# A two-layer decoder trunk on one core: both tiles' rotated transposes ahead of both splits, a longer softmax step, the residual loaded in eight pieces, and the first weights issued from ScalarE's queue

## The chip, the cores and the metric

The kernel runs on one core of a Trainium2 chip. The metric is the time of one execution in microseconds (us) on the device. The kernel before took 2349.48 us, the median of three runs (2347.7 to 2350.47).

## The reference

The program is a decoder trunk of two layers over a residual stream `x` of 256 rows by 2048 columns, in float32. The first layer uses differential attention with a partial rotary embedding, the second multi-head latent attention (MLA) with a separate rotated key. After each attention stands a cross-attention into 256 memory rows and an MLP with a squared ReLU. Each part starts with an RMS norm and ends with a residual addition.

```python
def partial_rope(x, cos, sin, rot):
    return jnp.concatenate([apply_rope(x[..., :rot], cos, sin), x[..., rot:]], axis=-1)

def diff_attention(h, wqkv, lam_vecs, subln, wo, cos, sin, lambda_init):
    q, k, v = jnp.split(h @ wqkv, 3, axis=-1)
    ...                                   # q, k: partial_rope, 16 half heads of 128
        s = jnp.where(causal_mask(q0, S), s, -jnp.inf)
        p = jax.nn.softmax(s, axis=-1)
        a = (p[:, :, 0] - lam * p[:, :, 1]).astype(v.dtype)
        return jnp.einsum('bhqk,bkhd->bqhd', a, v)

def mla_attention(h, wdown, q_norm, kv_norm, wuq, wukv, wo, cos, sin):
    d = h @ wdown
    c_q = rms_norm(d[..., :MLA_Q_LORA], q_norm)
    c_kv = rms_norm(d[..., MLA_Q_LORA:MLA_Q_LORA + MLA_KV_LORA], kv_norm)
    k_rope = apply_rope(d[..., MLA_Q_LORA + MLA_KV_LORA:][:, :, None, :], cos, sin)
    q = (c_q @ wuq).reshape(B, S, MLA_HEADS, MLA_NOPE + MLA_ROPE)
    q = jnp.concatenate([q[..., :MLA_NOPE], apply_rope(q[..., MLA_NOPE:], cos, sin)], axis=-1)
    ...                                   # k, v from c_kv, then softmax attention
```

## The kernel before

**Precision.** Each float32 operand is split into a rounded high part and a low part that is the rest. A product is three matmuls: high by high, high by low, low by high. For activations that come out of TensorE's transposes `split` makes the two parts: ScalarE casts the high part out of the result bank (L272), VectorE subtracts it from the bank to get the low part (L273).

**Weights.** They stream from HBM in tiles of 1 MB (`raw`), always loaded from SyncE's queue and in the order of the program. `split_weights` (L173) makes two halves of each: a cast on ScalarE gives `whi` (L187), a subtraction on VectorE `wlo` (L188). There are four `raw` buffers, which the tiles of the transposed input `xT` share at the start, and buffers of `whi` and `wlo` for two weight tiles. A half's cast therefore waits for the last matmul that reads the half two tiles earlier. `take` hands out the next weight tile, starts the load of a further one, and calls a hook if one is entered for the count of tiles taken so far.

**Matmuls.** `matmul_chunk` multiplies a chunk of four activation units by four weight tiles, into one result bank for each of the two row tiles of 128 rows (t = 0, 1). A weight tile is 24 matmuls of 128 x 512 (L155): two halves, two row tiles, six each. `w0`, `w1` and so on below are the weight tiles in the order of the stream; w0 to w3 give the first q chunk, w4 to w7 its k chunk, w8 to w11 its v chunk.

**Order.** TensorE runs its instructions in the order of the program. All else that it has to do (transposes L159, attention scores, products with the probabilities) is written as generators that `matmul_chunk` advances between its matmuls (`pump`), according to a planner's clock. A `yield` with a number of microseconds says when the next piece is due: `T_SM` (6.5) after a softmax, `T_ROT` (9.0) after a rotation, `T_TURN` (2.6) after a copy of transposed data. These figures are plans: they decide how many matmuls are put ahead of the next piece in TensorE's order, and how instructions are ordered on ScalarE, VectorE and GpSimd, each of which also works through its queue in order.

**The places that the change touches.**

- *Start.* SyncE loads `g`, then `xT` and w0 (in four pieces of 256 KB), w1, w2 between each other. `hooks[2] = first_norm` (L842) loads after the second tile the constants, both row tiles of `x` (1 MB each), positions and lambda vectors; ScalarE forms eight sums of squares (`sum_squares`, L301). From them come the scale of the norm (`rq`, `r1`) and, in `tables` (L677 to 707), the sine and cosine tables, of which sine needs another function table on ScalarE (L689).
- *Query heads of the first layer.* `project_diff` calls `heads_T` for each row tile: ScalarE evacuates and scales the bank (L354), GpSimd rotates a quarter of each head in six operations (`rope`, L365 to L370), TensorE transposes (L159), `split` makes the unit. In the code before, the scales and the tables are formed at the first of these calls.
- *Softmax step.* In `attend_diff` the difference of the two weighted probabilities `a` is formed on VectorE (L540, L541); after `yield T_SM + 1` TensorE transposes it (`prob_T`).
- *Rotated parts of MLA.* `shared_key` (one call) and `rotated` (in `project_latent`, one call for each of four head groups) rotate both row tiles, yield `T_ROT`, take a result bank `b`, and then do for each row tile in turn two transposes into its half of `b` and a `split` of that half.

Of the kernel before, what the change touches and what calls it, by code (L numbers as in the profile page):

```python
# [17 lines left out]
P = 128  # L18
D = 2048
S = 256  # L20
NT = 2
CH = 512
# [8 lines left out]
SC_DA = 1.0 / math.sqrt(128)  # L31
# [12 lines left out]
def trunk(ctx, tc, x, xT, mem, memT, positions, gcols, gfinal, lam_vecs, consts, W, out):  # L44
    nc = tc.nc
# [115 lines left out]
    def f32(ap):  # L161
        return ap.bitcast(F32)

    def load(dst, src):
        tc.keep_in_program_order(nc.sync.dma_start(dst, src))


    stream = []
# [1 line left out]
    def raw_tile():  # L170
        return wraw.tile([P, 4 * CH], F32, tag="raw", name=nm("raw"))

    def split_weights(src, width, pieces=2, loads=1):  # L173
        raw = raw_tile()
        n = 4 * width
        m = n // loads
        for i in range(loads):
            load(raw[:, i * m : (i + 1) * m], src[:, i * m : (i + 1) * m])
        m = n // pieces
        halves = []  # L180
        for i in range(pieces):
            at = i * m % (n // 2)
            if at == 0:
                halves.append([whalf.tile([P, 2 * CH], F32R, tag=tag, name=nm(tag)) for tag in ("whi", "wlo")])
            hi, lo = (w[:, at : at + m] for w in halves[-1])
            r = raw[:, i * m : (i + 1) * m]
            nc.scalar.copy(hi, r)  # L187
            nc.vector.tensor_tensor(lo, r, f32(hi), ALU.subtract)  # L188
        return halves

    plan = []
# [160 lines left out]
    def evacuate(ps, scale):  # L352
        e = work.tile([P, CH], F32, tag="ev", name=nm("ev"), bufs=6)
        nc.scalar.activation(e[:, : ps.shape[1]], ps, AF.Copy, scale=scale)  # L354
        return e
# [13 lines left out]
        e.tensor_tensor(a, m[0], m[1], ALU.subtract)  # L369
        e.tensor_tensor(b, n[0], n[1], ALU.add)  # L370

    def heads_T(ps, t, scale, dst, rot=None, spare=False):


        def task():
            e = evacuate(ps, scale)
            if rot:
                cos, sin, heads, half = rot
                rope(e.rearrange("p (h d) -> p h d", h=heads), cos, sin, heads, half)
            yield T_ROT if rot else T_EV  # L380
            b = ps
            if spare:
                b = yield from side_bank()
            split(dst, t, transpose4(e, b))
            if spare:
                give_back()
            yield T_TURN

        dst.run(task())
# [134 lines left out]
    def attend_diff(q, k, v, dst, coef, subcols):  # L524


        def block(t, heads, out):
            nk = (t + 1) * P
            sb = yield from side_bank()
            comps = [s for h in heads for s in (2 * h, 2 * h + 1)]  # L530
            scores(sb, [[(q, s, k[:, 0, s, :nk], k[:, 1, s, :nk])] for s in comps], nk, t, True)
            n = 2 * len(heads)
            pr, rs = softmax(sb, n)
            nc.vector.tensor_tensor(rs[:, :n], rs[:, :n], coef[:, :n], ALU.mult)
            a = work.tile([P, S], F32, tag="a", name=nm("a"))
            for i in range(len(heads)):
                p0 = pr[:, 2 * i * nk : (2 * i + 1) * nk]
                p1 = pr[:, (2 * i + 1) * nk : (2 * i + 2) * nk]
                ai = a[:, i * nk : (i + 1) * nk]
                nc.vector.tensor_scalar(ai, p1, rs[:, 2 * i + 1 : 2 * i + 2], None, ALU.mult)  # L540
                nc.vector.scalar_tensor_tensor(ai, p0, rs[:, 2 * i : 2 * i + 1], ai, ALU.mult, ALU.add)  # L541
            yield T_SM + 1
            pT = prob_T(a, 2, sb)
            give_back()
            yield T_TURN
            if not out:
                out.append((yield from side_bank()))
            po = out[0]
            nb = nk // P
            for i, h in enumerate(heads):  # L550
                for kb in range(nb):
                    blk = slice((i * nb + kb) * P, (i * nb + kb + 1) * P)
                    mm3(
                        po[:, h * S : (h + 1) * S], pT[:, 0, blk], pT[:, 1, blk],
                        val(v, 0, kb, h * S, S), val(v, 1, kb, h * S, S), kb == 0, kb == nb - 1,
                    )

        def normed(t, blocks, out):
            for b in blocks:
                yield b  # L560
            po = out[0]
            ss = small.tile([P, 2], F32, tag="ss2", name=nm("ss2"))
            for h in range(2):
                sum_squares(ss[:, h : h + 1], po[:, h * S : (h + 1) * S])
            r = rsqrt_mean(ss, 2, S)
            os = work.tile([P, CH], F32, tag="p", name=nm("os"), bufs=3)
            nc.vector.tensor_tensor(
                os.rearrange("p (h d) -> p h d", h=2), po.rearrange("p (h d) -> p h d", h=2),
                r[:, 0:2].unsqueeze(2).broadcast_to([P, 2, S]), ALU.mult,
            )  # L570
            yield T_NORM
            split(dst, t, scaled(transpose4(os, po), subcols))
            give_back()
            yield T_TURN

        def task():
            for i in q.tasks + k.tasks:
                yield i
            out = [[], []]
            b0 = Task(block(0, (0, 1), out[0]))  # L580
            yield 4.0
            b1 = Task(block(1, (0,), out[1]))
            n0 = Task(normed(0, [b0], out[0]))
            yield 4.0
            b2 = Task(block(1, (1,), out[1]))
            yield Task(normed(1, [b1, b2], out[1]))
            yield n0

        dst.run(task())
# [47 lines left out]


    load(g, gcols)
    warm = keep.tile([P, 1], F32, name="warm")  # L640
    nc.scalar.activation(warm, mhalf, AF.Exp)
    blank = work.tile([P, CH], mybir.dt.bfloat16, tag="junk", name="blank", bufs=1)
# [5 lines left out]
    norm = Stream(G_ATTN)  # L648
    for u in range(4):
        acts.append(given_unit(xT, u, G_ATTN))  # L650
        if u < 3:
            ready.append(split_weights(W["da_wqkv"][u], CH, 4 if u == 0 else 2, 4 if u == 0 else 1))
            plan.pop(0)
    posf = keep.tile([P, NT], F32, name="posf")
    cos = keep.tile([P, NT, NF], F32, name="cos")
# [8 lines left out]
    coef = keep.tile([P, 4], F32, name="coef")  # L664
    gsub = keep.tile([P, 4], F32, name="gsub")

    def first_norm():
        load(const, consts)
        for t in range(NT):
            load(xs[t], x[t * P : (t + 1) * P, :])  # L670
            for c in range(4):
                sum_squares(norm.ss[t][:, c : c + 1], xs[t][:, c * CH : (c + 1) * CH])
        load(pos, positions)
        load(lamv, lam_vecs)
        norm.rstd = [row_norm(norm.ss[t], D)[:, 0:1] for t in range(NT)]

    def tables():  # L677

# [160 lines left out]


    da_scales = []
    hooks[2] = first_norm  # L842

    hd = DA_ROT // 2

    def project_diff(gi):
        q, k, v = Held(unit()), Held(unit()), unit()
        for i, dst in enumerate((q, k)):
            ps = matmul_chunk(acts)
            if not da_scales:  # L850
                da_scales.append(keep2(norm.rstd, SC_DA, "rq"))
                da_scales.append(keep2(norm.rstd, 1.0, "r1"))
                tables()
            r = da_scales[i]
            for t in range(NT):
                heads_T(ps[t], t, r[t], dst, (cos[:, t, :hd], sin[:, t, :hd], 4, hd))
        ps = matmul_chunk(acts)
        for t in range(NT):
            values(ps[t], t, da_scales[1][t], v)
        return q, k, v  # L860
# [61 lines left out]
    def shared_key():  # L922
        for t in range(NT):
            e = ropes[t]
            rope(e[:, 0:1, 0:64], cos[:, t, hd:], sin[:, t, hd:], 1, hm)
            nc.vector.tensor_copy(e[:, 1, 64:128], e[:, 0, 0:64])
        yield T_ROT
        b = yield from side_bank()
        for t in range(NT):
            pt = b[:, 2 * t * P : 2 * (t + 1) * P]  # L930
            for i in range(2):
                flip(pt[:, i * P : (i + 1) * P], ropes[t][:, i, :])
            split(krope, t, pt.rearrange("p (k t) -> p k t", k=2))
        give_back()
        yield T_TURN

    def project_latent(gi):
# [3 lines left out]
        def rotated(ps):  # L941
            es = []
            for t in range(NT):
                e = evacuate(ps[t][:, :256], rq[t])
                rope(e[:, :256].rearrange("p (h d) -> p h d", h=4), cos[:, t, hd:], sin[:, t, hd:], 4, hm)
                es.append(e)
            yield T_ROT
            b = yield from side_bank()
            for t in range(NT):
                pt = b[:, 2 * t * P : 2 * (t + 1) * P]  # L950
                for i in range(2):
                    flip(pt[:, i * P : (i + 1) * P], es[t][:, i * P : (i + 1) * P])
                split(qr, t, pt.rearrange("p (k t) -> p k t", k=2))
            give_back()
            yield T_TURN

# [139 lines left out]
```

## Time and profile before

| | |
|---|---|
| median of the runs | 2349.48 us |
| the profiled execution | 2349.74 us |
| its span in the profile | 2348.0 us |
| mean granted TensorE clock | 0.992 |
| moved by DMA | 425.36 MB, mean 181 GB/s |

The profile is of one execution. Engines are PE (TensorE; PEld its weight loads), DVE (VectorE), ACT (ScalarE), POOL (GpSimd) and SP (SyncE). A row of the timeline gives the start in us from the start of the span, the duration, engine, line, operation, the tile written and the tile read with their sizes, and in brackets how long the engine was idle before and who released it. Several equal instructions in a row are put together (x4); their duration is then that of all. The chain of waits is followed back from the last instruction: its rows are start, duration, engine and line. The releaser is inferred, and where several semaphores were waited for, it is the one that came last in the records. PEclk is the share of TensorE's full clock that was granted.

### The profile page before, as it was taken

What the parts mean: (1) busy time and instruction counts of PE and PEld (TensorE: products, weight loads), DVE (VectorE), ACT (ScalarE), POOL (GpSimd) and SP (SyncE); (2) the same over time, 40 slices, a digit from 0 to 9 for tenths busy, and PEclk for the clock granted to TensorE, in tenths of its full rate; (3) what the DMA queues carried; (4) which work ended last, traced back from release to release, by engine and by line L of the source; (5) the groups of instructions that cost most, each with busy time, mean ns of one, the idle gap of its engine ahead of it and who ended that gap; (6) DMA issues with size and microseconds to landing.
All of it is one profiled execution on the core that took longest, in us unless ns stands there. A gap on an engine that the chain in (4) does not pass through costs nothing.

```text
span 2348.0 us, 27366 instructions
## 1 busy us (share of the span) xinstructions
PE 2306.8 (98%) x10860; PEld 1928.4 (82%) x10860; DVE 1302.3 (55%) x1502; ACT 1130.8 (48%) x1539; POOL 191.5 (8%) x258
## 2 busy tenths in 40 slices
PE   8999999999999999999999899999999999999998
PEld 6888787888888888888889688888888888888886
DVE  5665647774454454454556466777445445445454
ACT  6544545664434434434445455565443443443443
POOL 1111010001001000000001211000100100100111
PEclk9999999999999999999999899999999999999999
DMA  7455555545555555555545233554555555555553
GB/s 295 164 177 179 182 191 189 175 155 185 188 191 195 181 196 186 190 196 181 185 164 197 100 132 134 195 177 147 195 181 196 188 189 197 181 193 189 191 200 123
DMA packets 64353, 425.36 MB, mean 181 GB/s; under 512 B 7392, under 2 KB 7520, under 8 KB 15328
## 3 DMA queue, kind: packets, MB, share of 16 engines
q1 hardware_dynamic: 64224, 423.61, 53.0%
q8 instruction: 85, 1.39, 0.2%
q14 instruction: 44, 0.36, 0.0%
HBM read 421.48 MB, written 2.10 MB: 180 GB/s over the span
## 4 chain that ended last, share of the span: by engine, by line
PE 93%; DMA 2%; DVE 2%; ACT 1%; issue 1%; POOL 1%; SPq 0%; ACTq 0%; POOLq 0%; DVEq 0%
PE mm L155 88%; PE ax L155 2%; PE mm L159 2%; PE ax L159 1%; DVE wlo L188 1%; DMA memrow<-in_mem_dram 1%; ACT whi L187 1%; DMA x<-in_x_dram 0%; DMA raw<-in_da_wqkv_dram 0%; ACT junk L301 0%; DVE unit L295 0%; DVE unit L273 0%; DMA raw<-in_xT_dram 0%; POOL rope L367 0%; DMA raw<-in_memT_dram 0%
## 5 line engine op out<-in xcount | busy, mean ns | idle before, releaser
L155 PE MATMUL mm<-whi,unit 128*128 128x512 f32 (+2 forms) x6336 | 1978.2, 390 | 4.3 <-ACT whi L187 3.5
L188 DVE TENSOR_TENSOR wlo<-raw,whi 128x1024 fp32r<-128x1024 f32 (+2 forms) x794 | 962.6, 1213 | 943.9 <-ACT whi L187 943.0
L155 PEld LDWEIGHTS mm<-whi,unit 128*128 128x128 f32 x6336 | 1191.3, 189 | 242.6 <-ACT whi L187 4.8
L187 ACT CAST whi<-raw 128x1024 fp32r<-128x1024 f32 (+2 forms) x794 | 824.7, 1039 | 1056.4 <-PE mm L155 1036.1
L155 PE MATMUL mm<-wlo,unit 128*128 128x512 f32 (+2 forms) x3168 | 1228.8, 388 | 2.0 <-DVE wlo L188 2.0
L155 PEld LDWEIGHTS mm<-wlo,unit 128*128 128x128 f32 x3168 | 598.4, 189 | 118.0 <-DVE wlo L188 3.5
L813 POOL TENSOR_TENSOR ev<-ev 128x512 f32<-128x512 f32 x64 | 81.4, 1272 | 1160.4 <-ACT ev L812 1159.1
L349 DVE TENSOR_TENSOR x<-x,mm 128x512 f32<-128x512 f32 x144 | 94.9, 681 | 12.4 <-PE mm L155 12.1
L307 POOL TENSOR_TENSOR rs<-rs,mhalf 128x1 f32<-128x1 f32 (+1 forms) x28 | 21.2, 763 | 673.4 <-DVE rs L306 639.0
L273 DVE TENSOR_TENSOR unit<-mm,unit 128x512 fp32r<-128x512 f32 x88 | 56.5, 683 | 1.0 <-ACT unit L272 0.3
L272 ACT CAST unit<-mm 128x512 fp32r<-128x512 f32 x88 | 47.0, 586 | 6.1 <-PE mm L159 6.1
L812 ACT ACTIVATE ev<-mm,r 128x512 f32<-128x512 f32 x64 | 43.8, 685 | 11.4 <-PE mm L155 11.4
L409 ACT ACTIVATE p<-ax,nmax 128x256 f32<-128x256 f32 (+1 forms) x80 | 33.6, 427 | 31.0 <-DVE nmax L407 30.7
L159 PEld LDWEIGHTS mm<-const,ev 128*128 128x128 f32 x352 | 41.1, 140 | 5.7
L159 PE MATMUL mm<-const,ev 128*128 128x128 f32 x352 | 45.6, 272 | 0.0
L301 ACT ACTIVATE junk<-x 128x512 bf16<-128x512 f32 x56 | 35.2, 629 | 15.1 <-DVE x L349 13.0
L272 ACT CAST unit<-xg 128x512 fp32r<-128x512 f32 x52 | 31.9, 622 | 11.1 <-DVE xg L277 8.3
L155 PE MATMUL ax<-unit,unit 128*128 128x256 f32 (+1 forms) x240 | 37.2, 281 | 0.0
L273 DVE TENSOR_TENSOR unit<-xg,unit 128x512 fp32r<-128x512 f32 x52 | 35.7, 695 | 2.5 <-ACT unit L272 2.4
L155 PEld LDWEIGHTS ax<-unit,unit 128*128 128x128 f32 x240 | 34.4, 190 | 2.6
L365 POOL TENSOR_TENSOR rope<-ev,cos 128x64 f32<-128x64 f32 (+1 forms) x24 | 14.0, 584 | 251.4 <-ACT ev L354 250.5
L277 DVE TENSOR_TENSOR xg<-mm,g 128x512 f32<-128x512 f32 x40 | 26.1, 686 | 10.2 <-PE mm L159 10.2
(121 smaller groups left out, 620.3 us busy)
## 6 DMA issues: line engine op xcount, KB each, us to landing
raw<-in_mlp_wup_dram SPq DMA_DIRECT2D x128, 1024.0 KB, 5.0
raw<-in_mlp_wdown_dram SPq DMA_DIRECT2D x128, 1024.0 KB, 4.9
raw<-in_da_wqkv_dram SPq DMA_DIRECT2D x47, 1024.0 KB, 4.9
raw<-in_da_wo_dram SPq DMA_DIRECT2D x16, 1024.0 KB, 4.9
raw<-in_ca_wkv_dram SPq DMA_DIRECT2D x16, 1024.0 KB, 5.0
raw<-in_mla_wo_dram SPq DMA_DIRECT2D x16, 1024.0 KB, 4.9
raw<-in_ca_wq_dram SPq DMA_DIRECT2D x8, 1024.0 KB, 5.0
raw<-in_ca_wo_dram SPq DMA_DIRECT2D x8, 1024.0 KB, 4.9
```

The costliest lines, as they stand in the source:

```text
L155: return nc.tensor.matmul(o, stationary, moving, start=start, stop=stop)
L159: nc.tensor.transpose(o, src, ident)
L187: nc.scalar.copy(hi, r)
L188: nc.vector.tensor_tensor(lo, r, f32(hi), ALU.subtract)
L272: nc.scalar.copy(hi, src)
L273: nc.vector.tensor_tensor(dst[:, 1, :n, t * P : (t + 1) * P], src, f32(hi), ALU.subtract)
L277: nc.vector.tensor_tensor(tmp, src, cols.unsqueeze(2).broadcast_to([P, 4, P]), ALU.mult)
L301: nc.scalar.activation(junk[:, : src.shape[1]], src, AF.Square, accum_out=acc)
L349: nc.vector.tensor_tensor(xc, xc, ps, ALU.add)
L409: nc.scalar.activation(pr[:, i * w : (i + 1) * w], sb[:, i * w : (i + 1) * w], AF.Exp, bias=nmax[:, i : i + 1], accum_out=ssum[:, i : i + 1],)
L812: nc.scalar.activation(r, ps, AF.Relu, scale=rstd[t])
L813: nc.gpsimd.tensor_tensor(r, r, r, ALU.mult)
```

## The change

- `split_weights` and `load` can issue on another queue; w0 is now made ahead of the warm-up function on ScalarE and is issued, in its four pieces, from ScalarE's queue. w1 and w2 stay on SyncE's.
- The residual `x` is loaded in eight pieces of 128 x 512 of one row tile each instead of two loads of 128 x 2048. The hooks after the first to the sixth weight tile taken bring: constants; piece 0; piece 1; pieces 2 and 3; pieces 4 and 5; pieces 6 and 7 with positions, lambda vectors, the norm, the two scales and the tables.
- `heads_T` of the first layer's q and k can be handed a condition, `given`, and waits in the planner (in steps of 0.5) until the scales exist. On the device it is the semaphores that keep the order.
- The softmax step of `attend_diff` yields `T_SM + 3.5` in place of `T_SM + 1`.
- In `shared_key` and `rotated`, the four transposes of both row tiles are followed by the two splits; before it was two transposes, split, two transposes, split.

```diff
-    def split_weights(src, width, pieces=2, loads=1):
+    def split_weights(src, width, pieces=2, loads=1, queue=None):
...
-            load(raw[:, i * m : (i + 1) * m], src[:, i * m : (i + 1) * m])
+            load(raw[:, i * m : (i + 1) * m], src[:, i * m : (i + 1) * m], queue)
...
-    def heads_T(ps, t, scale, dst, rot=None, spare=False):
+    def heads_T(ps, t, scale, dst, rot=None, spare=False, given=None):
         def task():
-            e = evacuate(ps, scale)
+            while given and not given():
+                yield 0.5
+            e = evacuate(ps, scale() if given else scale)
...
-            yield T_SM + 1
+            yield T_SM + 3.5
             pT = prob_T(a, 2, sb)
...
     load(g, gcols)
+    ready.append(split_weights(W["da_wqkv"][0], CH, 4, 4, nc.scalar))
+    plan.pop(0)
     warm = keep.tile([P, 1], F32, name="warm")
...
-        if u < 3:
-            ready.append(split_weights(W["da_wqkv"][u], CH, 4 if u == 0 else 2, 4 if u == 0 else 1))
+        if 0 < u < 3:
+            ready.append(split_weights(W["da_wqkv"][u], CH))
             plan.pop(0)
...
+    def x_pieces(at, n):
+        for t, c in [(t, c) for t in range(NT) for c in range(4)][at : at + n]:
+            xc = xs[t][:, c * CH : (c + 1) * CH]
+            load(xc, x[t * P : (t + 1) * P, c * CH : (c + 1) * CH])
+            sum_squares(norm.ss[t][:, c : c + 1], xc)
+
     def first_norm():
-        load(const, consts)
-        for t in range(NT):
-            load(xs[t], x[t * P : (t + 1) * P, :])
-            for c in range(4):
-                sum_squares(norm.ss[t][:, c : c + 1], xs[t][:, c * CH : (c + 1) * CH])
+        x_pieces(6, 2)
         load(pos, positions)
         load(lamv, lam_vecs)
         norm.rstd = [row_norm(norm.ss[t], D)[:, 0:1] for t in range(NT)]
+        da_scales.append(keep2(norm.rstd, SC_DA, "rq"))
+        da_scales.append(keep2(norm.rstd, 1.0, "r1"))
+        tables()
...
-    hooks[2] = first_norm
+    hooks[1] = lambda: load(const, consts)
+    hooks[2] = lambda: x_pieces(0, 1)
+    hooks[3] = lambda: x_pieces(1, 1)
+    hooks[4] = lambda: x_pieces(2, 2)
+    hooks[5] = lambda: x_pieces(4, 2)
+    hooks[6] = first_norm
...
             ps = matmul_chunk(acts)
-            if not da_scales:
-                da_scales.append(keep2(norm.rstd, SC_DA, "rq"))
-                da_scales.append(keep2(norm.rstd, 1.0, "r1"))
-                tables()
-            r = da_scales[i]
             for t in range(NT):
-                heads_T(ps[t], t, r[t], dst, (cos[:, t, :hd], sin[:, t, :hd], 4, hd))
+                heads_T(
+                    ps[t], t, lambda i=i, t=t: da_scales[i][t], dst, (cos[:, t, :hd], sin[:, t, :hd], 4, hd),
+                    given=lambda: da_scales,
+                )
...
             for i in range(2):
                 flip(pt[:, i * P : (i + 1) * P], ropes[t][:, i, :])
-            split(krope, t, pt.rearrange("p (k t) -> p k t", k=2))
+        for t in range(NT):
+            split(krope, t, b[:, 2 * t * P : 2 * (t + 1) * P].rearrange("p (k t) -> p k t", k=2))
...
                 for i in range(2):
                     flip(pt[:, i * P : (i + 1) * P], es[t][:, i * P : (i + 1) * P])
-                split(qr, t, pt.rearrange("p (k t) -> p k t", k=2))
+            for t in range(NT):
+                split(qr, t, b[:, 2 * t * P : 2 * (t + 1) * P].rearrange("p (k t) -> p k t", k=2))
             give_back()
```

More of the change, by code (lines that the diff above doesn't have):

```diff
@@ L162, in f32, with load @@
         return ap.bitcast(F32)
-    def load(dst, src):
-        tc.keep_in_program_order(nc.sync.dma_start(dst, src))
+    def load(dst, src, queue=None):
+        tc.keep_in_program_order((queue or nc.sync).dma_start(dst, src))
     stream = []
```

## The prediction

> **What bounds the kernel now.** I read the page first, then the chain of waits, TensorE's waits, and the timeline around each long wait.
>
> ```profile
> span 2348.0 us, 27366 instructions
> PE 2306.8 (98%) x10860; PEld 1928.4 (82%) x10860; DVE 1302.3 (55%) x1502; ACT 1130.8 (48%) x1539; POOL 191.5 (8%) x258
> ```
>
> ```profile
> 2079.88 108.82 PE mm L155 x480
> ```
>
> TensorE is busy for 98% of the span, so time can only leave where it waits or runs slowly. From the chain's row an undisturbed matmul takes 108.82 / 480 = 0.2267 us; I call that one step. Apart from the moves below the number of matmuls and their order stay, so the prediction is a count of waits. TensorE's own list (waited for: us in total, times, longest):
>
> ```profile
> PE ax L159 <- DVE half L273: 17.3, 5, 6.0
> PE ax L159 <- ACT whi L187: 3.8, 1, 3.8
> PE mm L155 <- ACT whi L187: 3.5, 3, 2.6
> PE mm L155 <- DVE wlo L188: 2.0, 3, 1.0
> PE ax L159 <- DVE os L567: 1.5, 1, 1.5
> PE ax L159 <- DVE a L541: 1.4, 1, 1.4
> ```
>
> These six rows sum to 29.5 us. Behind some of them the clock was lowered. The next rows are stretches between the moments at which the granted clock changed (stretch, length, busy time of PE, PEld, DVE, ACT, POOL, then PEclk, DMA share, GB/s):
>
> ```profile
> 40.64:47.47 6.83, 5.82 (x13) 4.18 (x14) 5.13 (x6) 3.56 (x6) 5.87 (x10) 0.50 0.51 172
> 269.34:272.75 3.41, 2.72 (x8) 2.25 (x9) 3.09 (x10) 1.05 (x2) 0.00 (x0) 0.50 0.71 238
> 1296.75:1303.57 6.82, 4.65 (x12) 3.79 (x13) 2.15 (x5) 1.06 (x2) 0.27 (x2) 0.50 0.00 0
> 1310.40:1313.81 3.41, 3.41 (x13) 2.93 (x12) 1.81 (x3) 1.46 (x3) 0.00 (x0) 0.50 0.00 0
> 1334.29:1337.71 3.42, 3.42 (x10) 2.68 (x10) 1.12 (x2) 0.65 (x2) 0.00 (x0) 0.50 0.69 275
> 1399.15:1402.56 3.41, 3.37 (x9) 2.79 (x10) 0.42 (x1) 0.49 (x2) 0.00 (x0) 0.50 0.01 2
> 1457.17:1460.59 3.42, 2.98 (x8) 2.47 (x9) 0.71 (x2) 0.37 (x1) 0.00 (x0) 0.50 0.06 24
> ```
>
> Each follows a wait of 2.6 us or more; the waits of 1.4 and 1.5 us have none behind them. At half clock, half of the busy time is loss: a wait therefore has a second price, read from these rows. A page of the Trainium skill, "TensorE: Matmul & The Clock Gate" (Part 1: The HAM clock gate), has this as a rule: a free-running window of some 3.4 us, half rate after an idle one. The stretches of 3.41 us agree; as the window runs free, the page would let the same wait cost one window more or less in another run.
>
> **Part 1, both splits after all four transposes (the MLA layer).** The first and third of its five waits:
>
> ```profile
> 1291.66 1.25 PE L159 MATMUL ax<-const,ev 128*128 128x128 f32 x10
> 1293.36 0.45 POOL L370 TENSOR_TENSOR ev<-rope,rope 128x128 f32<-128x128 f32 x1
> 1293.38 0.39 ACT L272 CAST half<-ax 128x256 fp32r<-128x256 f32 x1
> 1297.05 0.20 DVE L926 COPY kr<-kr 128x64 f32<-128x64 f32 x1 [0.89 <-POOL kr L370]
> 1298.36 0.41 DVE L273 TENSOR_TENSOR half<-ax,half 128x256 fp32r<-128x256 f32 x1
> 1298.92 0.66 PE L159 MATMUL ax<-const,ev 128*128 128x128 f32 x2 [6.01 <-DVE half L273]
> 1330.35 0.90 POOL L370 TENSOR_TENSOR ev<-rope,rope 128x128 f32<-128x128 f32 x1
> 1333.54 0.41 PE L159 MATMUL ax<-const,ev 128*128 128x128 f32 x2 [2.78 <-DVE half L273]
> ```
>
> TensorE transposes tile 0, and the pair for tile 1, which goes to the same bank, starts only when VectorE has read tile 0's result out (1298.36 + 0.41). Data of tile 1 had been ready since 1293.81, the end of GpSimd's row. Without the split in between, the pair waits only for that: from 1292.91 (1291.66 + 1.25) to 1293.81 with some 0.3 to signal, so 1.2 is left of 6.01. At the third, TensorE is there at 1333.54 - 2.78 = 1330.76 and the rope ends at 1331.25: 0.8 left. For the fourth and fifth I take 0.1 each, as their rope had ended when TensorE came; and for the shared key nothing, whose copy at 1297.05 is done before TensorE, 3 us later, reaches it. Sum left: 2.2. The cover that makes this cheap is the rope being early; were it a microsecond late, each pair would lose that microsecond.
>
> What is late next: the splits, now ScalarE's cast and VectorE's subtraction for two tiles in a row, with the next k evacuation ahead and a weight cast behind. Scores read them a few matmuls later. One more such pair is 0.39 + 0.41 = 0.8 us in each of five groups; where the weight matmuls in between don't cover it, it is a wait. Between 0 (always covered) and 4.0 (never) I take 1.5, nearer the covered end, since tile 1's pair runs unnoticed behind such matmuls now. Lowered clock: all five stretches go, (4.65 + 3.41 + 3.42 + 3.37 + 2.98) / 2 = 8.9. Gain 17.3 - 2.2 - 1.5 + 8.9 = 22.5, with bounds 18 (4.0 for the splits and one lowered stretch left) and 24.
>
> **Part 2, the longer softmax step.** It puts the transposes of `a` 6 to 12 matmuls later in TensorE's order, in all four groups.
>
> ```profile
> 269.54 0.60 DVE L541 SCALAR_TENSOR_TENSOR a<-p,rsum,a 128x128 f32<-128x128 f32 x2
> 270.03 0.66 PE L159 MATMUL ax<-const,a 128*128 128x128 f32 x2 [3.75 <-ACT whi L187]
> ```
>
> The list names a weight cast, but what TensorE reads is `a`, and it went on as that row ended. Six steps are 1.4 us; the scores of the next heads, half-wide, now go ahead as well and take about 0.7, estimated as six half steps. Neither slows what makes `a`, so 3.75 falls to about 1.7. A wait of that size lowered no clock, so 2.72 / 2 = 1.4 goes too. The 1.41 at the second group goes wholly. The 1.5 for `os` stays: those transposes move by 12 steps, but so does the product that makes `os`. Matmuls that follow the moved transposes sooner may wait for the copy of their result; I take 0.5. Gain 2.05 + 1.4 + 1.4 - 0.5 = 4.3; bounds 1 (the clock falls all the same, the second wait turns up behind) and 6.
>
> **Part 3, the start.** Four things act together: w0 (the first weight tile; w1 and so on follow) is issued on ScalarE's queue, x arrives in 8 pieces between the weights, the norm's hook moves from the second to the sixth tile, and the tables follow it.
>
> ```profile
> 2.12 1.85 SPq L165 DMA_DIRECT2D raw<-in_da_wqkv_dram  x4
> 13.41 2.00 ACT L187 CAST whi<-raw 128x1024 fp32r<-128x1024 f32 x2 [1.47 <-DMA raw<-in_da_wqkv_dram]
> 20.00 11.46 DMA x<-in_x_dram
> 37.49 0.39 PE L155 MATMUL mm<-whi,unit 128*128 128x512 f32 x1
> 37.94 1.28 ACT L689 ACT_TABLE_LOAD   x1
> 39.43 1.97 ACT L187 CAST whi<-raw 128x1024 fp32r<-128x1024 f32 x2
> 40.51 0.70 PE L155 MATMUL mm<-whi,unit 128*128 128x512 f32 x1 [2.63 <-ACT whi L187]
> 41.49 0.67 ACT L354 ACTIVATE ev<-mm,rq 128x512 f32<-128x512 f32 x1
> 42.21 0.79 PE L155 MATMUL mm<-wlo,unit 128*128 128x512 f32 x1 [1.01 <-DVE wlo L188]
> 42.30 1.30 POOL L367 TENSOR_TENSOR rope<-ev,cos 128x64 f32<-128x64 f32 x1
> 47.59 0.32 POOL L370 TENSOR_TENSOR ev<-rope,rope 128x64 f32<-128x64 f32 x1
> 48.65 1.03 PE L159 MATMUL mm<-const,ev 128*128 128x128 f32 x8
> 56.12 0.62 PE L155 MATMUL mm<-whi,unit 128*128 128x512 f32 x2
> 56.55 1.05 ACT L187 CAST whi<-raw 128x1024 fp32r<-128x1024 f32 x1 [1.67 <-PE mm L155]
> ```
>
> Moving w0 takes four issues, 1.85 us, off SyncE's queue and puts them ahead of ScalarE's table load. The first wait after the first tile, at 13.41, is for w1, whose bytes stand behind the same ones as before: gain between 0 and 1.2, and I take 0.6. "Trainium Kernel Development and Optimization" in the Trainium skill (Key Constraints) speaks against more: queues of several engines share the same 16 DMA engines, and a second issuer saves issue time only. By it alone this gain would be 0 and the total 0.6 longer.
>
> What goes: x as two megabyte loads (11.46 us from issue to landing) ahead of w5, and 8 sums of squares plus a table load on ScalarE ahead of its cast. TensorE's gap 37.49 to 40.51 is 3.0 - 0.23 = 2.8 long, that to 42.21 1.5, the next 0.3, and half of 5.82, 2.9, is clock, of which I count 2.7: together 7.3.
>
> What comes: the instruction order has ScalarE do the second half of w8's cast, then tile 1's evacuation, the table load, sine and cosine. That cast overwrites a buffer which the 168th matmul reads last, and TensorE's transposes of the q heads, once behind the 138th matmul, stand right behind that 168th. So nothing hides the chain. Undisturbed, the 168th starts 48 steps after 37.49, at 48.4, less 0.6 is 47.8; the row at 56.55 shows a cast starting 0.43 after its matmul. Then: cast 1.0 (to 49.2), evacuation 0.7, table load 1.3 (51.2), sine 0.3, two small VectorE steps with signals 0.6, cosine 0.3 (52.4), and of twelve GpSimd operations the two done early left out, ten at 0.3 (55.5; 47.59's row), signal 0.2: TensorE resumes at 55.7. The eight transposes take 1.0; idle for 7.5 us, the clock will be lowered: one stretch costs 1.7, the two behind the 6.01 wait cost 4.65 / 2 = 2.3; I take 1.7. The next matmul is thus worth 55.7 + 1.0 + 1.7 = 58.4; before it was at 56.12 + 0.23 = 56.35. Net +2 us. If TensorE's clock stays up and the sine side of the rope runs early, -2. If GpSimd's operations take the 1.30 of the row at 42.30, as beside four VectorE subtractions, ten cost 10 us more: +12. I stay near the short end: in the new order VectorE has one subtraction there, done before the cosine.
>
> **The sum.** -22.5 - 4.3 + 2 = -24.8. The profiled execution took 2349.74 us (span 2348.0, 1.74 around it), within 0.3 of the median of the runs, 2349.48. Forecast 2349.74 - 24.8 = 2325 us.
>
> **Rivals.**
>
> The start wait vanishes altogether: the norm's work fits in ScalarE's free time and the q chain is ready at the 168th. For it: x lands earlier and ScalarE is 48% busy. Against: the cast of w8 can't precede that matmul. Then -7.3 - 0.6 instead of +2: 2349.74 - 22.5 - 4.3 - 7.9 = 2315.
>
> The rope is slow at the start, +12 instead of +2: 2335.
>
> The split's wait only moves: the three head groups' waits of some 2.8 us come back in front of the scores, with their clock, 3 x 2.85 + (3.42 + 3.37 + 2.98) / 2 = 13.4. Then 2325 + 13.4 = 2338. For it: VectorE's 0.41 still follows everything queued there, as at 1297.05 to 1298.77. Against: matmuls stand in between.
>
> Slower: after the new 7.5 us wait the clock doesn't come back, each following window having idle time in it, as 40.64 to 47.47 shows two in a row. A window at half clock costs 1.7; to eat 24.8 and another 4.7 takes 29.5 / 1.7, over 17 windows, about 59 us. With 25 such windows: 2325 + 1.7 x 25 = 2367. Against it: a slow TensorE leaves casts more time, and every lowered stretch here ended within two windows.
>
> No effect (each removed wait taken over by another): 2349.5; only if GpSimd is late by as much as VectorE was, which 1293.81 against 1298.77 contradicts.
>
> **How the numbers follow.** Forecast 0.55, start hidden 0.15, slow rope 0.12, split's wait moved 0.10, no effect 0.03, slower 0.05. The measurement can tell about 0.2%, 4.7 us, from no change: faster 0.92, same 0.03, slower 0.05. The range runs from just under the hidden start, 2313, to the moved wait, 2338; with edges lost, some 8 in 10.
>
> **What would show it.** Right: no wait of TensorE over 1.5 us in the MLA layer and no lowered clock between 1296 and 1460; one wait of some 2 us for `a` near 270; a wait of 7 us ahead of the q heads' transposes near 48 to 56, for GpSimd, in place of the one at 37 to 42. Wrong: waits for `half` in front of scores, or q transposes that start at 49.

## The result

The changed kernel took 2323.78 us, the median of four runs (2322.54 to 2324.55), against 2349.32 us before: a ratio of 0.9891, 95% interval 0.9874 to 0.9908. That is 25.5 us faster, with 21.6 to 29.6 us as the interval's ends. The forecast was 2325, range 2313 to 2338. The profiled execution is the first of the four, 2322.54 us, with a span of 2320.8; its span is 27.2 us shorter than the one before, where the sum of the prediction said 24.8. One execution of the last experiment below took 2868.24 us at a granted clock of 0.752; nothing here rests on it.

The page after, its first part:

```profile
span 2320.8 us, 27365 instructions
PE 2295.0 (99%) x10860; PEld 1920.4 (83%) x10860; DVE 1300.9 (56%) x1502; ACT 1131.7 (49%) x1539; POOL 188.5 (8%) x258
```

TensorE's list of what it waited for (us in total, times, longest), its first eight rows:

```profile
PE mm L159 <- POOL ev L370: 6.1, 2, 5.4
PE ax L159 <- DVE os L569: 1.7, 1, 1.7
PE mm L155 <- ACT unit L294: 1.6, 1, 1.6
PE ax L159 <- ACT whi L187: 1.5, 1, 1.5
PE ax L650 <- DVE blank L647: 1.2, 1, 1.2
PE ax L159 <- POOL ev L370: 1.0, 1, 1.0
PE mm L155 <- ACT unit L482: 0.9, 2, 0.4
PE mm L155 <- DVE wlo L188: 0.8, 1, 0.8
```

The row of 17.3 us for `half`, five waits, is gone; what stands in its place is one wait of 1.0 us for GpSimd and, further down the list, one of 0.5 (`PE ax L159 <- DVE pT L465: 0.5, 1, 0.5`), at the third place. The 3.8 us at the first softmax are 1.5, the 1.4 at the second are gone, `os` waits 1.7 where it waited 1.5. At the top is a new row of 6.1 us, the q heads' transposes at the start, where 3.5 and 2.0 us for `whi` and `wlo` stood. The row of 1.6 for `unit` ends at 7.70 us, ahead of the first matmuls of w0.

Stretches of the span (columns as before: stretch, length, busy times of PE, PEld, DVE, ACT, POOL, then PEclk, DMA share, GB/s):

```profile
51.66:58.49 6.83, 4.64 (x15) 3.66 (x16) 1.38 (x2) 1.41 (x3) 2.99 (x11) 0.50 0.33 138
269.34:272.75 3.41, 1.92 (x10) 1.62 (x10) 3.38 (x10) 1.87 (x6) 0.00 (x0) 1.00 0.51 142
1289.50:1296.30 6.80, 5.83 (x30) 4.74 (x29) 2.66 (x6) 2.50 (x6) 4.56 (x16) 1.00 0.46 154
1390.00:1460.00 70.00, 70.00 (x399) 60.84 (x398) 50.07 (x75) 40.91 (x83) 8.78 (x12) 1.00 0.47 158
```

Of the lowered stretches that the prediction lists only one at the start is left, and it has moved from 40.64 to 51.66, where it begins inside the new wait. (Both traces have another at the very end, from 2341.23 and 2314.70, after TensorE's last matmul.) To see where the time went I count the matmuls of the weight tiles in both traces and compare when the same one starts (the 241st is the first of w10, the 5001st lies ahead of the MLA layer's rotated parts, the 6201st behind them):

| matmul | before, us | after, us | gain since the row above |
|---|---|---|---|
| 169th, behind the q heads' transposes after the change | 56.35 | 55.73 | 0.6 |
| 241st | 73.56 | 74.36 | -1.4 |
| 1549th, end of the first layer's attention | 414.74 | 412.01 | 3.5 |
| 5001st | 1231.99 | 1229.23 | 0.0 |
| 6201st | 1561.34 | 1534.15 | 24.4 |
| 9504th, the last | 2338.82 | 2311.49 | 0.1 |

So the MLA part gave 24.4, the softmax step 3.5, and the start lost 0.8. No other stage moved.

The first of the five places in the MLA layer, after:

```profile
1288.89 1.25 PE L159 MATMUL ax<-const,ev 128*128 128x128 f32 x10
1290.61 0.46 POOL L370 TENSOR_TENSOR ev<-rope,rope 128x128 f32<-128x128 f32 x1
1291.12 0.44 PE L159 MATMUL ax<-const,ev 128*128 128x128 f32 x2 [0.97 <-POOL ev L370]
1291.60 0.37 ACT L272 CAST half<-ax 128x256 fp32r<-128x256 f32 x1 [0.87 <-PE ax L159]
```

Tile 1's pair starts 0.05 us after GpSimd's last operation for tile 1 and waits 0.97 us, where it had waited 6.01. At the third place the wait is 0.53, for a row of GpSimd that ends 0.05 us before the pair starts (1316.84 and 1316.89) and a copy of `pT` that ends as it starts; at the others none is left. Both splits now follow: ScalarE's cast starts at 1291.60, after both pairs.

The start, after:

```profile
47.39 0.39 PE L155 MATMUL mm<-whi,unit 128*128 128x512 f32 x1
47.52 0.15 DVE L735 TENSOR_SCALAR rq<-rs 128x1 f32<-128x1 f32 x1
47.81 1.04 ACT L187 CAST whi<-raw 128x1024 fp32r<-128x1024 f32 x1 [1.56 <-PE mm L155]
48.77 0.68 ACT L354 ACTIVATE ev<-mm,rq 128x512 f32<-128x512 f32 x1
49.46 1.28 ACT L698 ACT_TABLE_LOAD   x1
50.76 0.28 ACT L698 ACTIVATE sin<-ang 128x96 f32<-128x96 f32 x1
51.61 0.28 ACT L702 ACTIVATE cos<-ang 128x96 f32<-128x96 f32 x1 [0.57 <-DVE ang L701]
52.80 0.32 POOL L370 TENSOR_TENSOR ev<-rope,rope 128x64 f32<-128x64 f32 x1
53.18 1.12 PE L159 MATMUL mm<-const,ev 128*128 128x128 f32 x4 [5.40 <-POOL ev L370]
```

This is the chain that the prediction wrote down. ScalarE's second cast of w8 starts 0.42 us after the 168th matmul; evacuation, table load, sine, cosine and rope come one behind the other; TensorE stands still for 5.40 us, transposes tile 0 and waits another 0.7 (6.1 less 5.4) for tile 1.

### The profile page after: what moved, and what is told of

The parts are those of the page before. It is cut to its first block, busy times and chain, and to the rows that moved or that the text cites. A ratio compares the mean times of both kernels' runs of the same rounds, so it can differ in the third digit from the quotient of the medians.

```text
span 2320.8 us, 27365 instructions
## 1 busy us (share of the span) xinstructions
PE 2295.0 (99%) x10860; PEld 1920.4 (83%) x10860; DVE 1300.9 (56%) x1502; ACT 1131.7 (49%) x1539; POOL 188.5 (8%) x258
## 4 chain that ended last, share of the span: by engine, by line
PE 95%; DVE 1%; DMA 1%; ACT 1%; POOL 1%; issue 1%; ACTq 0%; SPq 0%; POOLq 0%
PE mm L155 89%; PE ax L155 2%; PE mm L159 2%; PE ax L159 1%; DVE wlo L188 1%; DMA memrow<-in_mem_dram 1%; DMA raw<-in_da_wqkv_dram 0%; ACT whi L187 0%; ACT junk L301 0%; POOL rope L367 0%; DVE x L349 0%; DVE nmax L409 0%; POOL ev L369 0%; POOL rope L366 0%; DVE unit L398 0%
## 5 line engine op out<-in xcount | busy, mean ns | idle before, releaser
L273 DVE TENSOR_TENSOR unit<-mm,unit 128x512 fp32r<-128x512 f32 x88 | 56.6, 684 | 5.2 <-ACT unit L272 4.5
L159 PE MATMUL mm<-const,ev 128*128 128x128 f32 x352 | 46.8, 276 | 6.1 <-POOL ev L370 6.1
L159 PEld LDWEIGHTS mm<-const,ev 128*128 128x128 f32 x352 | 41.6, 142 | 12.5 <-POOL ev L370 6.9
L411 ACT ACTIVATE p<-ax,nmax 128x256 f32<-128x256 f32 (+1 forms) x80 | 33.6, 428 | 22.9 <-DVE nmax L409 22.5
L273 DVE TENSOR_TENSOR unit<-xg,unit 128x512 fp32r<-128x512 f32 x52 | 35.7, 696 | 3.0 <-ACT unit L272 2.8
```

Of the source, the lines that this page charges most:

```text
L159: nc.tensor.transpose(o, src, ident)
L273: nc.vector.tensor_tensor(dst[:, 1, :n, t * P : (t + 1) * P], src, f32(hi), ALU.subtract)
L411: nc.scalar.activation(pr[:, i * w : (i + 1) * w], sb[:, i * w : (i + 1) * w], AF.Exp, bias=nmax[:, i : i + 1], accum_out=ssum[:, i : i + 1],)
```

## The experiments

Ten runs. Times are medians, and each is compared with runs of the kernel before on the same chip (2348.82, 2348.63 and 2349.95 us in three groups). The changed kernel itself was measured in a fourth group, with 2349.32 us before; a difference from it therefore goes across groups and is uncertain by about 1 us.

**The reordering alone.**

```diff
-            split(krope, t, pt.rearrange("p (k t) -> p k t", k=2))
+        for t in range(NT):
+            split(krope, t, b[:, 2 * t * P : 2 * (t + 1) * P].rearrange("p (k t) -> p k t", k=2))
...
-                split(qr, t, pt.rearrange("p (k t) -> p k t", k=2))
+            for t in range(NT):
+                split(qr, t, b[:, 2 * t * P : 2 * (t + 1) * P].rearrange("p (k t) -> p k t", k=2))
```

> The code before with the four transposes ahead of the two splits, and nothing else of the change. Theory (each MLA wait was a wait for tile 0's split, and goes with its lowered clock, independent of the other parts): TensorE's waits between 1290 and 1460 us fall to about 2 us in all, no lowered clock there, 24 us faster, near 2325 us; the wait at 37 to 42 us stays. Rival (the gain in the changed kernel needs the other parts, whose shifts made the ropes early): less than 18 us faster, above 2331 us, with waits for GpSimd of more than 4 us in all.

Measured: 2324.52 us, ratio 0.9896 (0.9881 to 0.9911), 24.3 us faster. Three rows of TensorE's list, the wait at the first softmax and what is left of the five waits:

```profile
PE ax L159 <- ACT whi L187: 4.2, 1, 4.2
PE ax L159 <- POOL ev L370: 1.0, 1, 1.0
PE ax L159 <- DVE pT L463: 0.5, 1, 0.5
```

1.0 us at the first of the five places and 0.5 at the third is all that is left of 17.3; the wait at the first softmax (here 4.2 us) stays, as it should. The gain doesn't need the other parts. One thing came otherwise than expected: the wait at 37 to 42 us did not stay. This trace has only 0.6 us there, but waits of 1.2 and 0.8 us at 13.77 and 15.49 and one of 2.1 us at 45.17, for GpSimd ahead of tile 1's q transposes, with lowered clock from 17.04 and from 47.76.

**The softmax step alone.**

```diff
-            yield T_SM + 1
+            yield T_SM + 3.5
```

> The code before with the longer softmax step alone. Theory: the wait of 3.75 us near 270 falls under 2 us and its lowered clock goes, the one of 1.4 near 369 goes, 3 to 4 us faster, near 2346 us. Rival (the transposes come later but so does everything that follows, so nothing is won): within 1 us of the kernel before.

Measured: 2344.87 us, ratio 0.998 (0.9971 to 0.9989), 4 us faster. The theory holds; the wait at the first group is 1.6 us and no lowered clock follows it.

**The start alone**, all of its edits and neither the softmax step nor the reordering.

```diff
+    ready.append(split_weights(W["da_wqkv"][0], CH, 4, 4, nc.scalar))
...
-    hooks[2] = first_norm
+    hooks[1] = lambda: load(const, consts)
+    hooks[2] = lambda: x_pieces(0, 1)
+    hooks[3] = lambda: x_pieces(1, 1)
+    hooks[4] = lambda: x_pieces(2, 2)
+    hooks[5] = lambda: x_pieces(4, 2)
+    hooks[6] = first_norm
```

> The code before with the start of the change alone: first weights on ScalarE's queue, x in eight pieces, the moved hook and tables. Theory (the wait at 37 to 42 us is replaced by one of the same size ahead of the q heads' transposes): the wait of 5 to 6 us near 48 to 53 us stands there and the time is the same or up to 2 us slower, 2349 to 2351 us. Rival (the start part helps and something else in the changed kernel costs): 4 us or more faster, below 2345 us.

Measured: 2351.97 us, ratio 1.0014 (1.0004 to 1.0023), 3.2 us slower (0.9 to 5.4), a little more than the theory's 2. TensorE's wait, from its list, and the stretch behind it:

```profile
PE mm L159 <- POOL ev L370: 6.1, 2, 5.4
```

```profile
50.30:60.54 10.24, 6.30 (x19) 4.94 (x20) 2.18 (x6) 2.58 (x5) 3.53 (x12) 0.50 0.29 104
```

The same wait, to a tenth, as in the changed kernel, and a lowered clock for 10.24 us, in which half of 6.30 was lost. In the order of before the waits vary more: in the trace of the softmax step alone, whose start has that order, they are 0.38 and 1.21 at 38 to 40 us instead of 2.63 and 1.01, and then 2.11 for GpSimd ahead of tile 1's q transposes, which the profile before doesn't have; no lowered clock follows. Four traces have the old order at the start. Their 241st matmul starts at 73.56 (before), 73.43 (the reordering alone), 71.39 (the softmax step alone) and 70.91 (the two banks, below), on average at 72.3; in the two traces with the new start and nothing else moved in, it is 74.36 and 75.54, on average 74.95. By these averages the new start costs 2.6 us, which agrees with the 3.2 of the runs. The profile before showed one of the slower draws of its start.

The three parts sum to -24.3 - 4.0 + 3.2 = -25.1 us, the whole change to -25.5: within the noise nothing shows that they act on each other.

**Only the first weights on ScalarE's queue.**

```diff
+    ready.append(split_weights(W["da_wqkv"][0], CH, 4, 4, nc.scalar))
+    plan.pop(0)
...
-        if u < 3:
-            ready.append(split_weights(W["da_wqkv"][u], CH, 4 if u == 0 else 2, 4 if u == 0 else 1))
+        if 0 < u < 3:
+            ready.append(split_weights(W["da_wqkv"][u], CH))
```

> The code before with only w0 issued from ScalarE's queue. Theory (the second tile's landing sets the start, not the issue): the first two tiles' matmuls gain 0 to 1 us and the time stays within 1 us of the kernel before. Rival (the four issues on SyncE hold everything back): w1 lands 1.8 us earlier and the wait ahead of the 25th matmul goes, 2 us faster.

Measured: 2348.57 us, ratio 0.9998 (0.9988 to 1.0007). What it does to the first three tiles:

```profile
12.10 1.99 ACT L187 CAST whi<-raw 128x1024 fp32r<-128x1024 f32 x2 [0.63 <-DMA raw<-in_da_wqkv_dram]
18.81 1.99 ACT L187 CAST whi<-raw 128x1024 fp32r<-128x1024 f32 x2 [3.10 <-DMA raw<-in_da_wqkv_dram]
```

w1's cast starts at 12.10 instead of 13.41, 1.3 us earlier, and the wait of 0.49 us ahead of the 25th matmul is gone, so the rival was right about w1. But w2's cast starts at 18.81, where it was 17.54: the wait is only handed on to the next tile, and the 73rd matmul, the first of w3, starts at 26.52 where it was 26.55. "Trainium Kernel Development and Optimization" of the Trainium skill (Key Constraints) says that queues share the 16 DMA engines and a second one saves issue time alone; a change that can't be told from none is what that leaves.

**A result bank of its own for tile 1's pair**, in the order of before.

```diff
-            b = yield from side_bank()
             for t in range(NT):
-                pt = b[:, 2 * t * P : 2 * (t + 1) * P]
+                b = yield from side_bank()
+                pt = b[:, : 2 * P]
...
-            give_back()
+                give_back()
```

(the same in `shared_key`)

> The code before, in its order (transposes, split, transposes, split), with a result bank of its own for tile 1's pair. Theory (the pair waited because tile 0's result was still being read out of the same bank): the five waits go as with the reordering alone, no lowered clock between 1290 and 1460 us, 22 to 25 us faster, near 2325 us. Rival (the order on ScalarE and VectorE holds the pair, whatever the bank): the waits for the split stay, within 2 us of the kernel before.

Measured: 2324.02 us, ratio 0.9895 (0.9881 to 0.9908): as much as the reordering gives.

```profile
1290.62 0.39 ACT L272 CAST half<-ax 128x256 fp32r<-128x256 f32 x1
1291.12 0.44 PE L159 MATMUL ax<-const,ev 128*128 128x128 f32 x2 [0.96 <-POOL ev L370]
1292.63 0.79 DVE L188 TENSOR_TENSOR wlo<-raw,whi 128x512 fp32r<-128x512 f32 x1
```

Tile 0's cast is still ahead of tile 1's pair, and its subtraction had not even begun when the pair ran (VectorE had waited for GpSimd's `kr` until 1292.48 and was then at other work until 1293.42), yet the pair waits for the rope alone. So it was the shared bank that tied the pair to the split. The wait was for a semaphore of the program (TensorE's list names VectorE's subtraction, `half` L273), which keeps a write of a result tile behind the reads of the same tile; whether it could be left out for disjoint columns was not tried.

**The q heads' transposes 36 matmuls later**, on top of the changed kernel.

```diff
-            yield T_ROT if rot else T_EV
+            yield (T_ROT if rot else T_EV) + late
...
-                    given=lambda: da_scales,
+                    given=lambda: da_scales, spare=i == 0, late=8.5 if i == 0 else 0,
```

> The changed kernel with the q heads' transposes of the first layer 36 matmuls later in TensorE's order, into side banks instead of the banks of their chunk. Theory (the new start wait costs 6.5 us of idle TensorE and 2.3 us of lowered clock, and only because nothing hides the chain): the wait near 48 to 55 us vanishes, the clock stays up, 7 to 9 us faster than the changed kernel, near 2316 us. Rival (ScalarE is late with everything by then, so the wait comes back in front of the next weight tiles' casts): under 3 us faster, above 2320 us, with waits for whi between 55 and 75 us.

Measured: 2315.40 us (2315.25 to 2316.07), 8.4 us faster than the changed kernel; the two traces differ by 6.5 us (spans of 2314.3 and 2320.8). The stretch:

```profile
47.50:58.50 11.00, 10.27 (x51) 8.38 (x50) 6.93 (x18) 8.07 (x11) 5.97 (x14) 1.00 0.58 190
```

TensorE works 10.27 of 11.00 us at full clock while the chain runs; no weight tile is late. The wait existed because nothing stood in front of the transposes.

**The tables early**, on top of the changed kernel.

```diff
+    def early_tables():
+        load(pos, positions)
+        load(lamv, lam_vecs)
+        x_pieces(0, 1)
+        tables()
...
-    hooks[2] = lambda: x_pieces(0, 1)
+    hooks[2] = early_tables
```

(and the two loads and `tables()` leave `first_norm`)

> The changed kernel with positions, lambda vectors and the tables at the second hook instead of the sixth. Theory (the chain behind w8's cast is long because the table load, sine, cosine and tile 0's rope stand in it): with tile 1's evacuation ahead of that cast and one rope of 1.9 us left, the wait shrinks from 6.5 to about 2 us and lowers no clock, 6 to 7 us faster than the changed kernel, near 2317 us. Rival (the chain is set by x landing in pieces, not by the tables): under 2 us faster.

Measured: 2315.83 us (2315.39 to 2316.01), 8.0 us faster than the changed kernel, where 6 to 7 was expected; the traces differ by 7.2 us.

```profile
46.18 0.68 ACT L354 ACTIVATE ev<-mm,rq 128x512 f32<-128x512 f32 x1
47.75 0.60 PE L159 MATMUL mm<-const,ev 128*128 128x128 f32 x4
47.95 1.04 ACT L187 CAST whi<-raw 128x1024 fp32r<-128x1024 f32 x1 [1.09 <-PE mm L155]
48.91 0.32 POOL L370 TENSOR_TENSOR ev<-rope,rope 128x64 f32<-128x64 f32 x1
49.29 0.66 PE L159 MATMUL mm<-const,ev 128*128 128x128 f32 x4 [0.93 <-POOL ev L370]
```

Tile 1's evacuation is ahead of w8's cast, tile 0's transposes run at once, and 0.93 us of wait is left, half of what was expected. The pieces of x still arrive as before, so it was the tables' place in ScalarE's order, not the pieces of x, that made the chain long.

**The wait filled with work nobody needs.** To price the clock by itself, matmuls on data at hand were put into the wait, their result left unread.

```diff
+            if pad is not None and t == 0:
+                filler = bank()
+                for _ in range(24):
+                    mmul(filler, pad[:, 0, 0, :P], pad[:, 0, 0:2, :].rearrange("p a b -> p (a b)"), True, True)
```

> The changed kernel with 24 matmuls of 128 x 512 whose result nobody reads put ahead of the q heads' transposes, 5.4 us of work in a wait of 5.4 us. Theory (the clock is lowered because TensorE stood idle): the chain ends at the same 53 to 55 us, no lowered clock follows, 1.7 to 2.5 us faster than the changed kernel, near 2321.5 us, although it does more work. Rival (the half clock has another cause, such as the transposes themselves): the stretch at 0.50 stays and the time is the same or up to 1 us slower.

Measured: 2339.53 us, 16 us slower than the changed kernel. The expectation missed a simple thing: the fill stood in all four head groups, and only the first has a wait. So the time says nothing about the clock. In its trace the clock stays at full rate from 5.69 to 282.17 us. It was run again with the fill in the first group alone.

> The filled wait again, with the 24 matmuls in the first of the four head groups alone; in the run before they stood in all four, and three of them filled no wait and cost 3 x 5.4 = 16.3 us. Theory (the clock is lowered because TensorE stood idle): no stretch at 0.50 near 50 to 60 us, 1.5 to 2.5 us faster than the changed kernel, near 2322 us. Rival (the half clock has another cause): the stretch stays, 2324 us or more.

Measured: 2321.64 us (2321.16 to 2322.55), 2.1 us faster than the changed kernel, although it does 5.4 us more work.

```profile
51.66:58.49 6.83, 5.70 (x29) 4.32 (x28) 1.86 (x4) 1.52 (x4) 3.57 (x12) 1.00 0.45 156
```

The same stretch that ran at 0.50 runs at 1.00. So the clock was lowered because TensorE stood idle, and the price here, 2.1 by the runs, is near half of the 4.64 us that TensorE was busy in it, 2.3. In the two traces the way from the 168th to the 241st matmul is 1.6 us shorter (25.35 against 26.97); 2.3 of clock less 0.5 of a longer wait for tile 1 (1.13 for 0.67) would be 1.8. "TensorE: Matmul & The Clock Gate" (Part 1: The HAM clock gate) in the Trainium skill has the rule of half rate after an idle window. The traces agree with it, though a window here needs to be idle only in part; the last section has the numbers.

**All of it together**, with longer steps for the waits that are left.

```diff
-            yield T_SM + 3.5
+            yield T_SM + 6
...
-            yield T_NORM
+            yield T_NORM + 2.5
...
-            yield T_ROT
+            yield T_ROT + 1.5
```

(the last in both rotated parts, with the early tables, and the q heads' transposes of the first group in side banks, `late=3.5`)

> The changed kernel with the early tables, the q heads' transposes 18 matmuls later into side banks, and three further steps lengthened: softmax to T_SM + 6, the norm of the heads to T_NORM + 2.5, the rotated parts to T_ROT + 1.5. Theory (what is left after the early tables are waits of 1.7, 1.7, 1.0 and 0.9 us that more matmuls in front hide): 4 to 6 us faster than with the early tables alone, near 2311 us. Rival (a later transpose only moves the wait to the product behind it): within 2 us of the early tables, 2314 to 2318 us.

Measured: 2310.84 us, ratio to before 0.9837 (0.9825 to 0.985), 13 us faster than the changed kernel and 5 faster than the early tables alone. TensorE's list begins:

```profile
PE mm L155 <- DVE wlo L188: 1.5, 2, 0.8
PE ax L650 <- DVE blank L647: 1.2, 1, 1.2
PE ax L155 <- DVE pT L425: 1.0, 3, 0.4
```

A little does move to the product behind the later transposes (1.0 us for `pT`, it was 0.6), but the waits of 1.7, 1.5, 1.0 and 6.1 us are gone.

## Why the prediction was right

*The MLA part* was forecast at 22.5 with an upper bound of 24 and gave 24.4 in the traces, 24.3 alone. Its mechanism is shown by the reordering alone and by the two banks. Two terms were off: the 1.5 us set aside for later splits did not come at all (no row of TensorE's list after the change names `half`), and of the 2.2 that was to be left 1.5 came, 0.97 at the first place (1.2 forecast), 0.53 at the third (0.8) and nothing at the others (0.2). With these two put right the prediction's own sum gives 17.3 - 1.5 + 8.9 = 24.7, against 24.4 measured. The upper bound of 24 was too tight because it set the splits at nothing but kept the whole 2.2.

*The softmax step* was forecast at 4.3; traces give 3.5, the runs alone 4.0. The first wait fell to 1.5 (1.7 forecast) and its lowered clock went, the second vanished, `os` grew by 0.3. The rows:

```profile
270.36 0.59 DVE L543 SCALAR_TENSOR_TENSOR a<-p,rsum,a 128x128 f32<-128x128 f32 x2
270.84 0.50 PE L159 MATMUL ax<-const,a 128*128 128x128 f32 x2 [1.49 <-ACT whi L187]
```

`a` is still what TensorE waits for: it goes on 0.48 us into the row of 0.59. Waits for `pT` give back 0.6, where 0.5 was counted. These terms sum to 2.3 + 1.4 + 1.4 - 0.3 - 0.6 = 4.2; the 0.7 between that and the 3.5 of the traces is in no row of the list, and stays open.

*The start* was forecast at +2 as a new wait in place of the old. Alone it measures +3.2 (0.9 to 5.4), in the pair of traces +0.8. The chain was right link by link: cast of w8, evacuation, table, sine, cosine, ten fast GpSimd operations. Forecast from 47.8, TensorE idle 7.5 us until all was rotated; measured from 47.39, 5.40 and 0.7, since tile 0's transposes ran ahead of tile 1's rope. The lowered clock took 2.3 rather than 1.7, which gives part of that back: 2 - 0.4 for the earlier start - 1.4 for the shorter waits + 0.6 is the 0.8 of the traces. The weak step is the old start's price, 7.3 us, taken from one execution, one of the two slowest of the four with that order. That is why the loss by the runs comes out above the loss between the two traces.

*The total* came within a microsecond of the forecast, and part of that is luck: the MLA part gave 1.8 more than its term, the start by the runs took 1.2 more, and the two largely cancel.

*Rivals.* The hidden start wait is refuted by the trace of the start alone; two small edits to the changed kernel produce it and give 8 us. The slow rope did not occur, as VectorE was free in that stretch. The moved split wait did not occur. The half clock that doesn't come back lasted two windows of 3.41 us in the changed kernel, three in the start alone, not seventeen. No effect at all is ruled out by the interval, 21.6 to 29.6 us.

## What to carry to other kernels

When two tiles share one result bank, put both tiles' writes ahead of both tiles' reads, or give each its bank: where, as here, the program holds a write of a tile behind the reads of the same tile, a read in between ties the second write to whatever stands in the reader's queue, here VectorE's and GpSimd's other work. A wait on the engine that bounds the kernel costs its length and, where some 2 us of idle time fall close together (the numbers follow), another 1.4 to 3 us of lowered clock, so waits of a microsecond that stand well apart are cheaper than one of the same sum. Spreading loads and norms over the start pays nothing if the work that depends on them lands in one in-order queue behind an instruction that waits for the bounding engine; look for what follows that instruction.

## What the runs showed of the hardware

VectorE can hold up GpSimd more sharply than the averages tell. In the kernel with the late heads, two rows of GpSimd and one of VectorE:

```profile
55.13 0.31 POOL L365 TENSOR_TENSOR rope<-ev,cos 128x64 f32<-128x64 f32 x1
55.22 1.30 DVE L188 TENSOR_TENSOR wlo<-raw,whi 128x1024 fp32r<-128x1024 f32 x1 [1.09 <-ACT whi L187]
55.41 1.30 POOL L366 TENSOR_TENSOR rope<-ev,sin 128x64 f32<-128x64 f32 x1
```

The first GpSimd operation had begun 0.09 us before VectorE's subtraction and takes 0.31 us; the next, of the same size, begins while the subtraction runs and takes 1.30. The subtraction ended at 56.52, GpSimd's operation at 56.71, so it does next to nothing until VectorE is done. Over the twelve traces of this case 192 of the 1152 operations of this size in the first layer's ropes took more than 0.45 us. Every one of them began while VectorE ran an operation with two inputs from SBUF; of the 233 that were under way when one of the weight subtractions began, none took more than 0.45. The "GPSIMD Engine Reference" of the Trainium skill (1. Specifications) lists GpSimd's SBUF interfaces as shared with VectorE, with contention when VectorE has two inputs from SBUF, which this subtraction does. The lesson for a sum is that a chain through GpSimd costs its fast time only in a stretch free of such subtractions. The chain of the late heads ended at 57.94 us, three microseconds later than in the changed kernel: 1.8 in two operations beside subtractions (1.18 and 1.30 in place of 0.32 each), the rest because the cosine came at 52.77 instead of 51.61. It cost nothing there, as matmuls stood in front.

The start differs between executions of the same instruction order: the wait ahead of the sixth tile was 2.63 us in one and 0.38 in another, and in a third there was none. A term that is read from a single execution at the start has that spread on it.

How long a wait is does not alone decide whether the clock is lowered. The wait of 2.11 us for GpSimd at the old start is in the trace of the reordering alone and in that of the softmax step alone, and only the first has a lowered clock behind it. The rows, one of the first and two of the second (columns as before):

```profile
44.35:47.76 3.41, 1.30 (x11) 0.91 (x9) 2.05 (x2) 0.66 (x2) 2.79 (x7) 1.00 1.01 404
42.76:46.18 3.42, 1.98 (x11) 1.35 (x9) 3.13 (x3) 1.65 (x2) 3.36 (x6) 1.00 0.86 352
46.18:49.59 3.41, 2.74 (x14) 2.37 (x15) 0.69 (x1) 1.25 (x2) 0.59 (x2) 1.00 0.53 223
```

In each trace all moments at which the clock changed lie on a grid of 3.413 us. In the first trace the wait falls into one window of that grid, with 2.11 us idle in it, and the next window runs at 0.50; in the second the edge at 46.18 divides it into 1.44 and 0.67, and the clock stays up. Laid on this grid, all twelve traces agree: behind each of the 31 windows at full clock in which TensorE was idle for 1.98 us or more the next one ran at 0.50, and behind each of the 8050 others, none with more than 1.74 idle, at 1.00. A lowered window was followed by another where TensorE was idle in it for about 0.7 us or more.
